# Where the last eight rows of five GpSimd loads go: pairs of rows on chosen DMA engines

## The chip, the cores and the metric

The kernel runs on one core of one Trainium2 chip. The metric is the device time of one execution in microseconds. Three executions of the kernel before took 792.04 to 793.46 us, with a median of 792.78 us.

## The reference, cut to what matters

```python
batch, seq, heads, dim = 16, 512, 16, 64          # q, k: float32 [16, 512, 16, 64]
q1, q2 = q[..., :32], q[..., 32:]                 # cos, sin: [512, 32], over all batches and heads
q_rot = np.concatenate([q1 * cos - q2 * sin, q1 * sin + q2 * cos], axis=-1)
...                                               # k_rot the same way
scores = np.einsum('bshd,bthd->bsht', q_rot, k_rot)   # float32 [16, 512, 16, 512]
```

Both inputs are rotated by position, and each query is multiplied with all 512 keys of its batch and head. The inputs have 33.6 MB each, the result 268 MB, so most of the traffic is the storing of scores.

## The kernel before, in words

**Tiles and staging.** A batch's 512 positions lie on 128 partitions, four neighbouring positions to a partition (`b (p c) h d`), so one load of q or k for a batch is 128 rows of 16 KB, 2 MB in all. The unit of the main loop is a tile: 128 queries (one c of one batch) against the 512 keys, for 16 heads. There are 64 tiles, i = 0 to 63, and tile i belongs to batch i // 4. The scores of a tile fill one staging tile `st`, 128 rows of 32 KB, and L188 stores it with one 4 MB transfer on SyncE's queue (SP). Three staging tiles exist, so ScalarE can begin tile i only when the store of tile i - 3 has landed. Batch 0 is treated in smaller pieces (`early`, L211), which the change does not touch.

**One tile.** In `for p in range(HP)` the function `scores` (L190) makes two matmuls for two heads (L201) and one ScalarE copy from PSUM into `st` (L208). Between them, written out by hand in the dictionary `tr`, stand the transposes (L170) of what later tiles need: at p = 1 and 3 those of q for tile i + 1, copied out by VectorE, and at p = 5 and 6 those of k for tile i + 4, copied out by ScalarE (L185). VectorE makes the rotation in three operations (L149, L150, L154): for q of tile i + 2 in the course of tile i, and at the end of tile i for k of tile i + 5. As every engine works in program order, q of batch b is first touched by VectorE around tile 4b - 2, and k of batch b at the end of tile 4b - 5; TensorE can't get past p = 5 of tile 4b - 4 without that k.

**Loads.** `load` (L113) is called at the end of tile i: q of batch i // 4 + 2 after a tile with i % 4 = 2, k of batch i // 4 + 3 after one with i % 4 = 3. Two buffers each are there for q and k, so a load waits for the last transposes of the batch two before. Most loads are one transfer on SP's queue behind the stores (L122).

**Five loads go through GpSimd.** `RELIEVED` (L74) names q of batches 6, 11 and 15 and k of batches 7 and 12. They go to `load_around` (L86), whose aim is that DMA engine 4 (`SLOW`) gets nothing of them. A transfer that GpSimd issues is spread from a cursor that runs over the 16 DMA engines. So `move_cursor` (L79) issues a tiny transfer of n rows of 16 bytes into `scratch`, which moves the cursor on by n, and `halves` (L94) then issues 120 rows, eight for each of 15 engines from engine 5 on. It cuts each row into two runs of 8 KB. The other eight rows go, for q, through SP (L111) to engines 0 to 7, and for k through GpSimd, with the cursor at 8, to engines 8 to 15, ahead of the 120 rows. In all GpSimd issues 18 transfers: 11 tiny ones, five of 120 rows and two of eight rows.

**Completions.** The framework gives GpSimd's transfers eight semaphores in turn. The ninth transfer takes the semaphore of the first and waits, on GpSimd, until the first has landed. GpSimd does nothing else in the main part of the kernel.

Of the kernel before, what the change touches and what calls it, by code (L numbers as in the profile page):

```python
# [10 lines left out]
def kernel(  # L11
# [8 lines left out]
    nc = tc.nc  # L20
    fp32 = mybir.dt.float32
# [3 lines left out]
    B, S, H, D = q.shape  # L25
    HD = D // 2
    P = 128
# [5 lines left out]
    const_pool = ctx.enter_context(tc.tile_pool(name="const", bufs=1))  # L33
# [37 lines left out]
    batches = {}  # L71

    RELIEVED = {("q", 6): 0, ("k", 7): 1, ("q", 11): 2, ("k", 12): 3, ("q", 15): 4}  # L74
    SLOW = 4
    scratch = const_pool.tile([P, 96], fp32, name="scratch")
    tiny = [0]

    def move_cursor(n):  # L79

        y = tiny[0]
        tiny[0] += 1
        src = bass.AP(q.tensor, 512 * y, [(512, n), (64, 2), (1, 2)])
        nc.gpsimd.dma_start(scratch[:n, 4 * y : 4 * y + 4].rearrange("p (a b) -> p a b", a=2), src)

    def load_around(which, b, t):  # L86

        n, E, F = 120, C * H * D, C * H * D // 2  # L90
        x = RELIEVED[which, b]
        d = dram[which][b]

        def halves(lo, hi):  # L94
            src = bass.AP(d.tensor, d.offset + lo * E + F, [(E, hi - lo), (-F, 2), (1, F)])
            v = t[lo:hi].rearrange("p c e -> p (c e)")
            dst = bass.AP(v.tensor, v.offset + F, [v.ap[0], (-F, 2), (1, F)])
            nc.gpsimd.dma_start(dst, src)  # L98

        if x == 0:  # L100
            nc.gpsimd.inc_swdge_sem([], [], mode="reset_dge_cursor")
        else:

            move_cursor(16 - SLOW)
        if x % 2:
            move_cursor(8)
            halves(n, P)
        move_cursor(SLOW + 1)
        halves(0, n)
        if not x % 2:  # L110
            nc.sync.dma_start(t[n:].rearrange("p c (h d) -> p c h d", h=H), d[n:])  # L111

    def load(which, b):  # L113

        if b >= B:
            return
        t = in_pool.tile([P, C, H * D], fp32, tag=which + "_in", name=which + "_sb")
        batches[which, b] = t
        if (which, b) in RELIEVED:
            load_around(which, b, t)  # L120
        else:
            nc.sync.dma_start(t.rearrange("p c (h d) -> p c h d", h=H), dram[which][b])  # L122
# [100 lines left out]
    with tc.manual_schedule():  # L223
# [15 lines left out]
        for i in range(C):  # L239
# [7 lines left out]
            for p in range(HP):  # L247
# [7 lines left out]
                if p in (2, 6):  # L255
                    m = len(dve) - (4 if p == 2 else 2) - (2 if i == C - 1 else 0)
# [64 lines left out]
```

## Time and profile before

| | |
|---|---|
| median of three executions | 792.78 us |
| the profiled execution | 792.13 us |
| its span, first to last instruction | 790.4 us |
| DMA traffic | 336.18 MB, mean 425 GB/s |
| DMA queue 1 (SP), share of 16 engines | 96.4%, 325.46 MB |
| DMA queue 0 (GpSimd), share of 16 engines | 3.1%, 10.10 MB |
| TensorE busy / ScalarE / VectorE / GpSimd | 684.4 / 562.0 / 544.7 / 11.9 us |
| one 4 MB store, issue to landing, median | 24.7 us |
| one 2 MB load of k on SP, issue to landing, median | 28.3 us |
| 120 rows of q / of k on GpSimd, issue to landing, median | 27.8 / 43.3 us |

The span and the busy times come from one profiled execution, which itself took 792.13 us; 1.7 us of that lie outside the span. "Issue to landing" is the time from the start of the issuing instruction until the last of 16 completion marks, and so includes the wait behind transfers that were issued earlier. Times in the traces are counted from the span's start.

### The profile page before, as it was taken

Reading aid. Unit: us, or ns where it says so; the run is one execution under the profiler, and the core shown is the slowest. Engines: PE = TensorE matmul, PEld = TensorE weight load, DVE = VectorE, ACT = ScalarE, POOL = GpSimd, SP = SyncE. Lnnn points to the kernel's source line nnn. Section 1 sums busy time; section 2 is a strip of 40 time slices with the busy share of each in tenths; the row PEclk is TensorE's granted clock in tenths of the full one; section 3 lists DMA queues with packets and bytes.
Section 4 is the critical chain, followed back from the end, with each engine's and each line's share of the span. In section 5 each row is a group of like instructions: output and inputs, shape, how many; then the busy total and the mean of one; then the engine's idle time right before and its main releaser. Section 6 shows DMA issues by size and latency. Waiting matters only on the chain.

```text
span 790.4 us, 7750 instructions
## 1 busy us (share of the span) xinstructions
PE 684.4 (87%) x3072; PEld 296.4 (38%) x3072; DVE 544.7 (69%) x516; ACT 562.0 (71%) x647; POOL 11.9 (2%) x24
## 2 busy tenths in 40 slices
PE   4989998988988889798996989889899798799960
PEld 2444443433433334343342433334334343344420
DVE  6999988666766678576785767667678487587400
ACT  3888886865857768486785866777577586588770
POOL 0000000000001000000000001000000000000000
PEclk9999999998999999898998989999899899899995
DMA  9999999999999999999999999999999999999997
GB/s 357 417 425 439 429 430 435 425 435 436 429 429 428 413 432 419 433 423 438 433 427 436 426 432 429 422 432 424 430 432 427 436 429 432 430 432 434 432 429 340
DMA packets 18836, 336.18 MB, mean 425 GB/s; under 512 B 2312, under 2 KB 3592, under 8 KB 4616
## 3 DMA queue, kind: packets, MB, share of 16 engines
q1 hardware_dynamic: 16704, 325.46, 96.4%
q0 software_dynamic: 1808, 10.10, 3.1%
q8 instruction: 24, 0.39, 0.2%
q10 hardware_dynamic: 288, 0.13, 0.1%
q14 instruction: 12, 0.10, 0.0%
HBM read 67.24 MB, written 268.44 MB: 425 GB/s over the span
## 4 chain that ended last, share of the span: by engine, by line
DMA 49%; PE 40%; ACT 5%; DVE 3%; issue 1%; ACTq 0%; SPq 0%; DVEq 0%
DMA out_dram<-st 46%; PE ps L201 30%; PE bank L170 10%; ACT st L208 5%; DMA q_sb<-in_q_dram 2%; DVE part L149 1%; DMA early<-in_k_dram 1%; DVE q_sb L150 0%; DVE k_sb L154 0%; DVE k_sb L150 0%; DVE q_sb L154 0%; DVE early L150 0%; DVE kT_t L185 0%; ACTq L316 0%; DVE early L154 0%
## 5 line engine op out<-in xcount | busy, mean ns | idle before, releaser
L208 ACT COPY st<-ps 128x1024 f32<-128x1024 f32 x512 | 495.7, 1020 | 192.6 <-DMA out_dram<-st 109.8
L201 PE MATMUL ps<-kT_t,qT_t 64*128 64x512 f32 x2048 | 544.0, 649 | 67.0 <-ACT st L208 67.0
L201 PEld LDWEIGHTS ps<-kT_t,qT_t 64*128 64x128 f32 x2048 | 183.6, 196 | 256.2 <-issue 133.3
L185 DVE COPY qT_t<-bank 128x512 f32<-128x512 f32 x118 | 81.6, 691 | 193.9 <-PE bank L170 193.9
L170 PEld LDWEIGHTS bank<-ident,q_sb 128*128 128x128 f32 x480 | 54.2, 149 | 99.0 <-issue 96.4
L170 PEld LDWEIGHTS bank<-ident,k_sb 128*128 128x128 f32 x480 | 50.3, 140 | 96.4 <-DVE k_sb L150 39.5
L170 PE MATMUL bank<-ident,q_sb 128*128 128x128 f32 x480 | 85.1, 304 | 0.9 <-PE ps L201 0.9
L170 PE MATMUL bank<-ident,k_sb 128*128 128x128 f32 x480 | 78.5, 286 | 1.6 <-DVE qT_t L185 1.2
L185 ACT COPY kT_t<-bank 128x512 f32<-128x512 f32 x122 | 72.4, 598 | 6.4 <-PE bank L170 6.4
L154 DVE TENSOR_TENSOR k_sb<-k_sb,part 128x1024 f32<-128x1024 f32 x60 | 73.5, 1225 | 2.1
L150 DVE TENSOR_TENSOR q_sb<-q_sb,cos_t 128x1024 f32<-128x1024 f32 x60 | 73.5, 1225 | 2.1
L150 DVE TENSOR_TENSOR k_sb<-k_sb,cos_t 128x1024 f32<-128x1024 f32 x60 | 73.5, 1225 | 2.0
L149 DVE TENSOR_TENSOR part<-q_sb,ss_t 128x1024 f32<-128x1024 f32 x60 | 73.5, 1225 | 2.0
L149 DVE TENSOR_TENSOR part<-k_sb,ss_t 128x1024 f32<-128x1024 f32 x60 | 73.0, 1216 | 0.9 <-DMA k_sb<-in_k_dram 0.7
L154 DVE TENSOR_TENSOR q_sb<-q_sb,part 128x1024 f32<-128x1024 f32 x60 | 72.9, 1216 | 0.0
L170 PE MATMUL bank<-ident,early 128*128 128x128 f32 x64 | 10.5, 315 | 12.4 <-DVE early L154 10.5
L170 PEld LDWEIGHTS bank<-ident,early 128*128 128x128 f32 x64 | 8.3, 161 | 17.4 <-issue 13.4
L149 DVE TENSOR_TENSOR part<-early,ss_t 128x1024 f32<-128x1024 f32 x8 | 9.8, 1222 | 5.8 <-DMA early<-in_k_dram 5.7
L98 POOL DMA_DIRECT2D q_sb<-in_q_dram x3 | 2.3, 752 | 620.2 <-PE bank L170 446.2
L154 DVE TENSOR_TENSOR early<-early,part 128x512 f32<-128x512 f32 x16 | 10.3, 687 | 0.2
L150 DVE TENSOR_TENSOR early<-early,cos_t 128x1024 f32<-128x1024 f32 x8 | 9.8, 1225 | 0.3
L185 ACT COPY qT_t<-bank 128x512 f32<-128x512 f32 x10 | 5.7, 629 | 3.2 <-PE bank L170 3.2
(12 smaller groups left out, 15.9 us busy)
## 6 DMA issues: line engine op xcount, KB each, us to landing
out_dram<-st SPq DMA_DIRECT2D x60, 4096.0 KB, 24.7
k_sb<-in_k_dram SPq DMA_DIRECT2D x13, 2048.0 KB, 28.3
q_sb<-in_q_dram SPq DMA_DIRECT2D x12, 2048.0 KB, 26.5
out_dram<-st SPq DMA_DIRECT2D x16, 1024.0 KB, 13.8
q_sb<-in_q_dram POOLq DMA_DIRECT2D x3, 1920.0 KB, 27.8
k_sb<-in_k_dram POOLq DMA_DIRECT2D x2, 1920.0 KB, 43.3
early<-in_k_dram SPq DMA_DIRECT2D x1, 1536.0 KB
early<-in_q_dram SPq DMA_DIRECT2D x1, 1536.0 KB
```

Source lines behind the costliest of these rows:

```text
L98: nc.gpsimd.dma_start(dst, src)
L149: nc.vector.tensor_tensor(pv, xs, ss, op=mult)
L150: nc.vector.tensor_tensor(xc, xc, cs, op=mult)
L154: nc.vector.tensor_tensor(y, y, z, op=add)
L170: nc.tensor.transpose(bank[:, x, :], src, ident)
L185: copy(out=dst, in_=src)
L201: nc.tensor.matmul(out=po, lhsT=lhs[64 * r : 64 * r + 64, :], rhs=rh, start=True, stop=True)
L208: nc.scalar.copy(out=so, in_=si)
```

## The change

The eight rows leave SP and the fixed groups of engines. Each load now issues its 120 rows first, from engine 5 on, and then four transfers of two rows, each to two neighbouring engines; the table gives the first engine of each pair. A transfer starting at 7 goes to engines 7 and 8, one at 15 to 15 and 0, one at 2 to 2 and 3, one at 9 to 9 and 10. Before each of them stands the tiny transfer that moves the cursor there (two tiny ones, of nine and eight rows, where it has to move by one; none where it stands right). GpSimd now issues 53 transfers: 28 tiny ones, five of 120 rows and 20 of two rows. `scratch` becomes wider for the greater number of tiny transfers.

```diff
-    RELIEVED = {("q", 6): 0, ("k", 7): 1, ("q", 11): 2, ("k", 12): 3, ("q", 15): 4}
-    SLOW = 4
-    scratch = const_pool.tile([P, 96], fp32, name="scratch")
+    RELIEVED = {
+        ("q", 6): (7, 15, 7, 15),
+        ("k", 7): (7, 9, 15, 2),
+        ("q", 11): (7, 15, 2, 7),
+        ("k", 12): (7, 9, 15, 2),
+        ("q", 15): (7, 15, 7, 15),
+    }
+    SLOW, NE = 4, 16
+    scratch = const_pool.tile([P, 224], fp32, name="scratch")
     tiny = [0]
+    cursor = []
...
         n, E, F = 120, C * H * D, C * H * D // 2
-        x = RELIEVED[which, b]
         d = dram[which][b]

-        def halves(lo, hi):
+        def rows(lo, hi, engine):
+            d_n = (engine - cursor[0]) % NE
+            for m in (9, 8) if d_n == 1 else (d_n,) if d_n else ():
+                move_cursor(m)
             src = bass.AP(d.tensor, d.offset + lo * E + F, [(E, hi - lo), (-F, 2), (1, F)])
             v = t[lo:hi].rearrange("p c e -> p (c e)")
             dst = bass.AP(v.tensor, v.offset + F, [v.ap[0], (-F, 2), (1, F)])
             nc.gpsimd.dma_start(dst, src)
-
-        if x == 0:
+            cursor[0] = (engine + min(hi - lo, NE - 1)) % NE
+
+        if not cursor:
             nc.gpsimd.inc_swdge_sem([], [], mode="reset_dge_cursor")
-        else:
-
-            move_cursor(16 - SLOW)
-        if x % 2:
-            move_cursor(8)
-            halves(n, P)
-        move_cursor(SLOW + 1)
-        halves(0, n)
-        if not x % 2:
-            nc.sync.dma_start(t[n:].rearrange("p c (h d) -> p c h d", h=H), d[n:])
+            cursor.append(0)
+        rows(0, n, SLOW + 1)
+        for x, engine in enumerate(RELIEVED[which, b]):
+            rows(n + 2 * x, n + 2 * x + 2, engine)
```

## The prediction, made before the changed kernel was run

> **What bounds the kernel now.** I read the page's slices first, then its chain, the waits, and the timelines of GpSimd and VectorE.
>
> ```profile
> DMA  9999999999999999999999999999999999999997
> GB/s 357 417 425 439 429 430 435 425 435 436 429 429 428 413 432 419 433 423 438 433 427 436 426 432 429 422 432 424 430 432 427 436 429 432 430 432 434 432 429 340
> ...
> DMA 49%; PE 40%; ACT 5%; DVE 3%; issue 1%; ACTq 0%; SPq 0%; DVEq 0%
> ```
>
> The 16 DMA engines are busy from the first slice to the last, at a flat rate: the kernel ends when the slowest engine has moved its bytes. The chain's 40% PE does not contradict this; it passes through matmuls that themselves waited for staging tiles, as the waits show:
>
> ```profile
> POOL q_sb L98 <- PE bank L170: 446.2, 2, 224.0
> ...
> ACT st L208 <- DMA out_dram<-st: 109.8, 42, 5.7
> ...
> DVE part L149 <- DMA k_sb<-in_k_dram: 0.7, 1, 0.7
> ```
>
> ScalarE waits 109.8 us for stores; loads make VectorE wait 0.7 us. So compute runs ahead, by the stores in flight: one lands 24.7 us after issue and moves in 9.7 (8 packets of 1.21 per engine), so about 2.5 are queued. When are the relieved loads issued and used? GpSimd, then VectorE:
>
> ```profile
> 226.37 0.75 POOL L98 DMA_DIRECT2D q_sb<-in_q_dram  x1 [223.98 <-PE bank L170]
> 227.12 1.13 POOL L84 DMA_DIRECT2D scratch<-in_q_dram  x2
> 246.84 0.57 POOL L98 DMA_DIRECT2D k_sb<-in_k_dram  x1 [18.59 <-PE bank L170]
> 247.41 0.57 POOL L84 DMA_DIRECT2D scratch<-in_q_dram  x1
> 247.97 0.76 POOL L98 DMA_DIRECT2D k_sb<-in_k_dram  x1
> ```
> ```profile
> 290.31 1.23 DVE L149 TENSOR_TENSOR part<-k_sb,ss_t 128x1024 f32<-128x1024 f32 x1
> ```
> ```profile
> 535.23 1.23 DVE L149 TENSOR_TENSOR part<-k_sb,ss_t 128x1024 f32<-128x1024 f32 x1 [0.72 <-DMA k_sb<-in_k_dram]
> ```
>
> By the trace's completion marks the 120 rows of k7 landed at 290.19, those of k12 at 535.11: VectorE takes both within 0.12 us. **The relieved k loads have no slack.** The q loads have some: q6 landed at 255.2 and is first used at 268.35.
>
> **What the skill says.** "DMA: Bandwidth & Descriptors", section "Queues, rings and completion order": an engine alternates between the queues that have work, packet by packet. The packet records agree: beside a 32 KB store packet of 1.213 us, an 8 KB packet of queue 0 (0.309) comes every 1.52 us, and even a tiny one every 1.22. Same page, "Why a DMA increments its semaphore by 16 and not by 1": GpSimd's transfers post a completion on all 16 engines whatever their shape, and a small one uses consecutive engines from a cursor. Queue 0 has 400 packets of 4 bytes, 16 for each of 18 transfers and 112 that fill engines without data in the large ones; so every small transfer costs every engine turns. "Latency and other measured facts" calls engines 7 and 15 usually slower; the change puts most rows there. The records carry no engine number, so this trace can't confirm it.
>
> **The price of a small transfer.** Landings before (last mark): q6's 120 rows 255.24, the tiny ones of 12 and 8 rows 257.66 and 259.63, k7's eight rows 263.51, a tiny one 265.93, k7's 120 rows 290.19. The ring serves strictly in order: 2.3 us for a tiny one, 3.9 with data, 24.3 for 120 rows. Two-row pieces do not occur before. Bounds: the tiny one's 2.3 and the eight-row piece's 3.9 (also two 8 KB packets per engine used); I take 3.9.
>
> **The change, part by part.**
>
> *Removed from SP:* three eight-row issues (about 1 us each). SP idles 659.7 us at L188 for ScalarE: 0. *GpSimd's issue time:* 35 more transfers at 0.57 are 20 us on an idle engine: 0 by itself.
>
> *Tiny packets:* 17 more tiny transfers with 2 packets and 18 more data pieces with up to 3, at some 10 ns each, are 0.9 us per engine at most, on the bound.
>
> *Rows moved.* A row is 0.62 us. Before, engines 0 to 7 got 3 of the 40 rows and 8 to 15 got 2. After: 7 and 8 get 8; 15 and 0 get 7; 2 and 3 get 3; 9 and 10 get 2; the rest none. So 8 carries +3.7 us, 7 and 15 +3.1, 0 +2.5; 1, 4, 5, 6 carry -1.9, 11 to 14 -1.2. Sorting the packet records into 16 chains (each packet starts 3 or 4 ns before its forerunner ends), five end between 784.95 and 785.68, eleven between 788.07 and 790.37, on average 787.97. Perfect evening is worth 2.4 us; if the last engine is 2, 3, 9 or 10, nothing.
>
> *Order and waits.* The changed program's order on GpSimd names the wait of each transfer. q6: 120 rows, tiny, pair, tiny, pair, tiny, pair, tiny, then the last pair, which takes the semaphore of the 120 rows: **it is not issued before they land, and GpSimd, in order, holds k7 behind it.** k7's 120 rows then wait for q6's first pair, and its own last pair for its own 120 rows; likewise q11, k12 and q15. Working it out from the landings above:
>
> - q6: 120 rows 255.2; four tiny and three pairs, 9.2 + 11.7 = 20.9, give 276.1; last pair 280.0, against first use at 268.35. VectorE stops 12 us in tile 22, and behind it the copies of q of tile 23, so TensorE stops at p = 5. Then products 2.5, a copy 0.7 and some 4 to the store: 287 instead of 282.0. Store 21 lands at 296.25, so the engines have work: 0 (5 us if that cover were gone).
> - k7: 120 rows released at 261.4 (q6's first pair) and not at 248; in the ring behind everything to 280.0 and a tiny one, 282.3; +24.3 is 306.6; four tiny and three pairs 327.5; last pair 331.4. While the SP loads of q7 and k8 pass (16 KB packets of 0.61), turns are shorter: 4.8 us for q7's eight packets, about half of that for k8's. I take **324**, instead of 290.2.
> - What is late next: k's rotation 3.7, then tile 24 from p = 5 to its store, about 5: store 24 at 333, not 306.44, its first packet 2 later. SP's queue then holds nothing beyond k8's load, whose 16 marks fall between 322.0 and 325.9: dry from 324 to 335, 11 us. If k7 lands at 318, 5; at 326, when the empty SP queue stops holding the ring up, 13. I take 9.5.
> - q11: two more tiny ones stand ahead of its 120 rows, 499.9 + 4.6 = 504.5; five tiny and four pairs give 531.6 (first use 514.2): store 42 near 539, covered by store 41. k12: 533.9 + 24.3 + 24.8 = 583 without short turns, as late against 535.2 as k7 or more: another 9.5.
> - q15: 698.9 + 24.8 = 723.7, used at 709.8: store 58 near 731, when store 57 lands (731.3): 0 to 3, I take 1.
>
> A dry spell is lost for good: every tile needs 10.0 us of compute against 12.1 of DMA with loads, 9.7 without, so engines can't make it up. It also puts the 16 engines in step again, so I take the rows' evening (-2.4 to +1.5) and the tiny packets (+0.9) together at 0.
>
> Sum: 792.13 + 9.5 + 9.5 + 1 = 812.1 us against the profiled execution, which is 0.65 below the median; I forecast **812**.
>
> **Rivals.**
>
> *Not slower: the late pieces stay under the queue's cover.* k7 can land up to 313 (324 less 2, 5 and 3.7) and nothing runs dry. With pairs at 2.3 us, k7 would end at 275.9 + 24.3 + 18.4 = 318.6, less the short turns 7.2: 311. Then only evening and tiny packets count: 792.1 - 2.4 + 0.9 = 790.6, or up to 793 if the last engine isn't relieved. For it: the chain ends so uneven, and 2.5 stores are queued. Against it: the eight-row piece took 3.9, and k's slack is nil. 12%.
>
> *Slower still:* each dry spell 13, and q6 or q15 uncovered too (5 and 3): 792 + 34 = 826. Against it: stores 21 and 57 were in flight. 10%.
>
> *The rows don't go where the table says* (the pairs on other engines): evening fails, the waits stay; the same 812.
>
> **How the numbers follow.** Forecast (803 to 820) 73%, covered 12%, slower still 10%, one spell only (794 to 803) 5%. 0.2%, 1.6 us, is about what a measurement of this kernel can tell from no change: faster 0.07 (the covered case with evening), same 0.05, slower 0.88. Range 795 to 822.
>
> **What would show it.** Right: DMA slices below 9 near 325 to 335 and again some 250 us later; VectorE's L149 on k_sb waiting tens of us; GpSimd's pairs waiting for DMA; the last pair of k7 landing near 324; stores 24 and 44 some 25 us late. Wrong: DMA at 9 throughout and k7 landed by 313; or the loss found as longer packets.

## The result, and the profile after

The changed kernel takes 822.58 us (median of 6 runs, 821.33 to 823.79) against 792.64 for the kernel before in the same session: a ratio of 1.0375, with a 95% interval of 1.0358 to 1.0391. It is slower, as forecast, but by 30 us and not by 20: 10.6 us above the forecast of 812, and 0.6 beyond the range's end. The profiled execution took 821.37 us with a span of 819.6, 29.2 more than before. One run further below, 818.36 us of the kernel with the pairs first, counts as slow and is left out of that kernel's median and ratio.

The page's slices and its chain, in the changed kernel (a slice is 20.5 us here):

```profile
DMA  9999999999999998699999999999499999999998
GB/s 353 420 425 439 431 428 435 431 435 427 435 423 433 423 379 352 283 409 412 432 422 441 421 430 429 428 407 410 204 434 383 432 425 439 414 433 431 431 427 365
...
DMA 50%; PE 30%; DVE 9%; issue 4%; ACT 3%; POOL 1%; ACTq 0%; DVEq 0%; POOLq 0%
```

The row of nines has two holes, at 320 to 340 and at 580 to 600 us. They are what the prediction called dry spells. The GB/s row shows more than the digits do: 379 stands *ahead* of the first hole, in a slice whose digit is 9, so the engines count as busy there and move less. The chain now passes through VectorE (9%), and 4% of it is "issue", time for which the profile shows no wait.

The waits of VectorE, in us: total, how often, longest. Before, its waits for k loads were 0.7 us.

```profile
DVE part L153 <- DMA scratch<-in_q_dram: 37.9, 2, 27.6
DVE part L153 <- DMA k_sb<-in_k_dram: 28.0, 1, 28.0
DVE part L153 <- DMA q_sb<-in_q_dram: 20.0, 2, 10.6
```

Two waits of about 28 us are those for k7 and k12, three of about 10 those for q6, q11 and q15. One k wait and one q wait are put down to `scratch`: a tiny transfer next to the last pair ended about when it did, and the wait goes to what came last by the profile. The timelines of VectorE and of SP in the changed kernel, then of SP in the kernel before (start, duration, what it waited for):

```profile
279.49 1.23 DVE L153 TENSOR_TENSOR part<-q_sb,ss_t 128x1024 f32<-128x1024 f32 x1 [10.58 <-DMA q_sb<-in_q_dram]
...
321.08 1.23 DVE L153 TENSOR_TENSOR part<-k_sb,ss_t 128x1024 f32<-128x1024 f32 x1 [27.59 <-DMA scratch<-in_q_dram]
```
```profile
260.81 28.56 SPq L192 DMA_DIRECT2D out_dram<-st  x3
289.47 1.42 SPq L126 DMA_DIRECT2D q_sb<-in_q_dram  x1
299.05 0.33 SPq L192 DMA_DIRECT2D out_dram<-st  x1
299.48 1.09 SPq L126 DMA_DIRECT2D k_sb<-in_k_dram  x1
333.95 10.35 SPq L192 DMA_DIRECT2D out_dram<-st  x2
```
```profile
296.42 0.33 SPq L188 DMA_DIRECT2D out_dram<-st  x1
296.86 1.07 SPq L122 DMA_DIRECT2D k_sb<-in_k_dram  x1
306.44 27.01 SPq L188 DMA_DIRECT2D out_dram<-st  x3
```

k7 is used at 321.08, 30.8 us later than before. After k8's load, issued at 299.48, SP issues nothing until 333.95, when store 24 comes (before: 306.44). That load, the last thing in its queue, lands between 323.96 and 325.75.

Where do 29.2 us lie? I added up all packet records and divided by 16. Per engine, time without a packet grew from 2.1 us to 22.6, **20.5 us of dry time**; time with a packet grew from 788.3 to 797.0, **8.7 us of longer or additional packets**, though the bytes are the same. The windows view shows both kinds (columns: window, length, busy of each engine with instruction counts, PEclk, DMA share, GB/s; a packet counts where it starts, so a share can pass 1); first the changed kernel, then the kernel before:

```profile
290.00:292.00 2.00, 2.00 (x11) 0.70 (x9) 2.00 (x3) 1.48 (x2) 0.00 (x0) 1.00 1.02 287
292.00:294.00 2.00, 2.00 (x12) 1.11 (x12) 0.90 (x2) 1.42 (x3) 0.00 (x0) 1.00 1.05 254
...
320.00:340.00 20.00, 12.00 (x52) 5.45 (x52) 18.47 (x18) 8.07 (x10) 0.00 (x0) 0.72 0.52 222
```
```profile
290.00:292.00 2.00, 2.00 (x9) 0.53 (x5) 1.91 (x3) 0.77 (x1) 0.00 (x0) 0.82 0.95 410
292.00:294.00 2.00, 2.00 (x13) 1.07 (x12) 1.97 (x2) 1.91 (x4) 0.00 (x0) 1.00 1.03 442
```

At 290 to 294 the DMA share is full in both kernels, yet only 254 to 287 GB/s pass, against 410 to 442. At 320 to 340 half of the engines' time is empty. Of the 8.7 us, by packet size and place: 2.3 between 280 and 300 and 1.4 between 540 and 560 (k's 8 KB rows, and some stores beside them); 2.1 between 360 and 380 and 1.9 between 620 and 640 (a store and a load some 30 us after each dry spell); 1.1 in tiny and other small packets.

### The profile page after: what moved, and what is told of

Same layout as the page of the kernel before. It is cut to its first block, busy times and chain, and to the rows that moved or that the text cites. A ratio compares the mean times of both kernels' runs of the same rounds, so it can differ in the third digit from the quotient of the medians.

```text
span 819.6 us, 7794 instructions
## 1 busy us (share of the span) xinstructions
PE 677.6 (83%) x3072; PEld 295.9 (36%) x3072; DVE 543.4 (66%) x516; ACT 561.1 (68%) x647; POOL 31.9 (4%) x59
## 4 chain that ended last, share of the span: by engine, by line
DMA 50%; PE 30%; DVE 9%; issue 4%; ACT 3%; POOL 1%; ACTq 0%; DVEq 0%; POOLq 0%
PE ps L205 23%; DMA out_dram<-st 22%; DMA k_sb<-in_k_dram 15%; DMA q_sb<-in_q_dram 7%; PE bank L174 7%; DMA scratch<-in_q_dram 6%; DVE part L153 3%; ACT st L212 3%; DVE early L154 1%; DVE k_sb L158 1%; DVE k_sb L154 1%; DVE early L158 1%; DVE q_sb L154 1%; POOL q_sb L107 1%; DMA sin_t<-in_sin_dram 0%
## 5 line engine op out<-in xcount | busy, mean ns | idle before, releaser
L205 PE MATMUL ps<-kT_t,qT_t 64*128 64x512 f32 x2048 | 534.8, 641 | 42.4 <-ACT st L212 42.1
L205 PEld LDWEIGHTS ps<-kT_t,qT_t 64*128 64x128 f32 x2048 | 181.7, 193 | 223.7 <-issue 140.6
L174 PE MATMUL bank<-ident,k_sb 128*128 128x128 f32 x480 | 82.0, 295 | 65.3 <-DVE qT_t L189 65.3
L174 PEld LDWEIGHTS bank<-ident,k_sb 128*128 128x128 f32 x480 | 52.4, 145 | 161.5 <-DVE qT_t L189 71.1
L107 POOL DMA_DIRECT2D q_sb<-in_q_dram x15 | 9.0, 602 | 580.4 <-PE bank L174 353.9
L92 POOL DMA_DIRECT2D scratch<-in_q_dram x28 | 16.2, 578 | 50.9 <-DMA q_sb<-in_q_dram 37.7
L158 DVE TENSOR_TENSOR early<-early,part 128x512 f32<-128x512 f32 x16 | 10.3, 687 | 0.2
```

The source lines that it names most:

```text
L158: nc.vector.tensor_tensor(y, y, z, op=add)
L174: nc.tensor.transpose(bank[:, x, :], src, ident)
L205: nc.tensor.matmul(out=po, lhsT=lhs[64 * r : 64 * r + 64, :], rhs=rh, start=True, stop=True)
```

## The experiments

The prediction's theory, **R**: GpSimd's ring (its packets waiting at the DMA engines) is served in order, one packet to a turn beside the stores; the small transfers make q6 and then k7 late; when k is later than the queue's cover (the stores and loads still in flight), SP's queue runs dry. Its rivals: **P**, the placement on engines 7, 8, 15 and 0 costs by itself; **W**, the semaphore wait of the last pair is what makes it late, not the ring's sum. Later a question was added: what makes packets longer (8.7 us).

### Small transfers without any row moved

Two kernels: the kernel before, with rows where they were, and 14 or 6 tiny transfers without use behind the 120 rows of q6 and q11.

```diff
+    EXTRA = 14
...
         halves(0, n)
+        if which == "q" and b < 15:
+            for _ in range(EXTRA):
+                move_cursor(8)
```

> The kernel before with its rows where they were; behind the 120 rows of q6 and of q11 stand 14 more tiny cursor transfers of eight rows, which carry no data of the computation. Theory R (GpSimd's ring serves its transfers one after the other, 2.3 us for a tiny one, and k lands behind all of them): k7 lands near 290.2 + 14 x 2.3 = 322, less some 5 where SP loads shorten the turns, so 317 to 320; the DMA engines run dry for 4 to 10 us at k7 and again at k12, 800 to 815 us in all. If the longer packets seen in the changed kernel follow from a dry spell, the load after each spell shows them here too, about 2 us each. Rival P (the loss comes from where the rows go, engines 7, 8, 15 and 0): 792 to 794, as no row moves.

> The same with 6 tiny transfers instead of 14. Theory R: k7 lands near 290.2 + 14 = 304, which is later than before but earlier than 313, where the stores in flight stop covering it: no dry spell, 791.5 to 794 us. A loss in proportion to the transfers (a cost of the tiny packets themselves) would give 6/14 of what 14 cost, 796 to 802. Rival P: 792 to 794.

Measured: with 14, 824.04 us (ratio 1.0387, 1.0372 to 1.0403); with 6, 796.46 (1.0039, 1.0025 to 1.0054). With 14, k7 landed at 322.65 and VectorE used it as late as in the changed kernel:

```profile
322.77 1.23 DVE L153 TENSOR_TENSOR part<-k_sb,ss_t 128x1024 f32<-128x1024 f32 x1 [35.39 <-DMA k_sb<-in_k_dram]
```

With 6 it landed at 305.15, VectorE waited 14.0 and 17.0 us for the k loads, and still no dry spell followed (3.1 us without a packet in the whole run). Both times lie above what R had put down (800 to 815 and 791.5 to 794). The 796.46 lies at the edge of the range for a loss in proportion to the transfers, 796 to 802; but 6/14 of the 30.4 us that 14 really cost would be 13, and 2.8 were lost. They are longer packets too (3.3 us in the profiled execution). With 14, the whole loss comes without a single row on another engine: P is not needed for it, and small transfers in k's way are enough. With 14, the dry time is 16 us, and 15.7 us are longer packets; I had not expected those. Between 300 and 311 q7's load on SP and k7's rows ran at once there, with hardly a store beside: 16 KB packets took about 1000 ns instead of 611, 8 KB packets 410 to 530 instead of 309.

### Each half of the change alone

In one kernel q has pairs and k stays as before; in the other k has pairs and q stays. The table of engines, left out here, has 0 or 8 for a load that stays.

```diff
...
+        if RELIEVED[which, b] == 8:
+            rows(n, P, 8)
         rows(0, n, SLOW + 1)
+        if RELIEVED[which, b] == 0:
+            nc.sync.dma_start(t[n:].rearrange("p c (h d) -> p c h d", h=H), d[n:])
+        elif RELIEVED[which, b] != 8:
+            for x, engine in enumerate(RELIEVED[which, b]):
+                rows(n + 2 * x, n + 2 * x + 2, engine)
```

> q6, q11 and q15 send their last eight rows in pairs as in the changed kernel; k7 and k12 send theirs as before, in one transfer to engines 8 to 15 ahead of the 120 rows. Theory R: k7 lands near 279.4 + 2.3 + 3.9 + 2.3 + 24.3 = 312, less 5 for short turns: 307 to 310, under 313, so no dry spell: 790 to 794 us. Rival P: engines 7, 8, 15 and 0 get 5 to 8 of the rows, nearly what they get in the changed kernel: 806 or more. A loss in proportion to the number of small transfers would also give about 806.

> k7 and k12 send their last eight rows in pairs as in the changed kernel; q6, q11 and q15 send theirs through SP as before. Theory R: q6 lands as before near 255, k7's 120 rows near 282 and its last pair near 303 to 307, under 313: no dry spell, 790 to 794 us, though neither half of the change alone is free of late landings. Rival P and a loss in proportion to the number of small transfers: half of the change's loss, about 806.

Measured: pairs for q, 797.41 us (1.0047, 1.0032 to 1.0062); pairs for k, 794.43 (1.0016, 1.0007 to 1.0024). k7 landed at 309.21 and 304.89. Neither has a dry spell (2.1 and 3.3 us without a packet). R had put both at 790 to 794, so the first is 3.4 us too slow and the second 0.4; P and a loss in proportion, at about 806, are far off. Together the halves lose 0.6%, the whole change 3.75%: it is the *sum* of both delays that passes a limit. In the kernel with pairs for q the lost time is in longer packets again: 6.1 us in its profiled execution, 4.9 of them in 8 KB packets, at 475 to 590 ns on average between 288 and 296.

### The placement alone, and a smaller dose

The first kernel gives pairs to q15 only, where no relieved k follows. The second sends one pair to 7 and 8 and one to 15 and 0 for each q, the other four rows through SP, and leaves k as before. Its edit, without the table:

```diff
...
+        if which == "k":
+            rows(n, P, 8)
         rows(0, n, SLOW + 1)
+        if which == "q":
+            nc.sync.dma_start(t[n + 4:].rearrange("p c (h d) -> p c h d", h=H), d[n + 4:])
```

> Only q15 sends its last eight rows in pairs, to engines 7, 8, 15 and 0; the other four loads send theirs as before. No k load stands behind it, so theory R has no dry spell. It measures the evening alone, with the engines' lead kept to the end: engines 1 to 6 get one row less, 7, 8, 15 and 0 one or two more; 0 to 1 us less than before if the last engine is one of 1 to 6, otherwise the same: 791.5 to 794. Rival P (rows on 7, 8, 15 and 0 slow these engines): 8 of 40 rows, 6 us slower, 798 or more.

> For q6, q11 and q15 one pair of rows to engines 7 and 8 and one to 15 and 0 through GpSimd, after the 120 rows, and the other four rows through SP; k7 and k12 as in the kernel before (their eight rows ahead). Worked out from the ring's order and prices: q6 complete at 267.6, just within its use at 268.35; k7 near 300 instead of 290, late by 10 against a limit of 20 or so: no dry spell. If that holds, 791 to 795, with at most 1 us gained by the evening. If the placement itself costs, or small transfers cost even where nothing is late, above 797.

Measured: 793.38 us for the first (1.0003, 0.9995 to 1.0011), 793.26 for the second (1.0000, 0.9992 to 1.0008). In the second, q6's last row landed at 267.37 and VectorE did not wait for it; k7 landed at 298.29 with a wait of 11.4 us, and nothing ran dry. So rows on the engines that the table calls 7, 8, 15 and 0 cost nothing that can be measured, at 8 and at 12 rows of the 30 that the changed kernel puts there. P had put even 8 rows at 6 us, and the two halves together move all the rows for 0.6%: P falls. Which engine a row really went to, no record tells. The rows bring nothing either. The last 30 us of the first kernel have 2.84 us without a packet instead of 3.65, so its chains end 0.8 us more evenly, but q15's pairs are late too and leave 1.9 us dry at 720 to 740.

### The pairs ahead of the 120 rows

The changed kernel with the order turned round. No pair then has to wait for the 120 rows of its own load.

```diff
-        rows(0, n, SLOW + 1)
         for x, engine in enumerate(RELIEVED[which, b]):
             rows(n + 2 * x, n + 2 * x + 2, engine)
+        rows(0, n, SLOW + 1)
```

> The changed kernel with each load's four pairs ahead of its 120 rows and not behind them. The last pair no longer takes the semaphore of the 120 rows, so no pair waits for them; the ring carries the same transfers. Theory R: the sum of the ring is the same, k7 lands last with its 120 rows, near 325: 820 to 828 us. Rival W: the waits of 23 to 25 us on GpSimd are gone, so the loss goes to half or less, under 808.

Measured: 804.89 us, widely spread (802.86, 804.89 and 812.87; 1.0174, 1.0126 to 1.0223). By the number W is right (under 808), and R's 820 to 828 misses. But the long wait did not go, as was expected; it moved. k7's last pair now takes the semaphore of q6's 120 rows, and k7's 120 rows stand behind it:

```profile
280.77 0.56 POOL L107 DMA_DIRECT2D k_sb<-in_k_dram  x1 [24.59 <-DMA q_sb<-in_q_dram]
...
289.26 0.76 POOL L107 DMA_DIRECT2D k_sb<-in_k_dram  x1 [3.08 <-DMA k_sb<-in_k_dram]
```

Here the waits do bind for some 2 us: when k7's 120 rows are issued at 289.26, SP's queue is empty too, and the DMA share at 288 to 290 is 0.29. Until about 296 the ring then had hardly a turn to share with stores, about half of the 120 rows moved by then, and k7 landed at 313.21 and not near 325, with no dry spell behind it. This execution, the fastest, lost 3.5 us without a packet, at 280 to 300 and at 540 to 560, and 7.3 us in longer packets. So the run does not decide between R and W for k7. For q6, none of whose transfers waits for its 120 rows any more, it does: q6 was used at 280.56, no earlier than in the changed kernel (279.49). For the changed kernel itself GpSimd's timeline decides:

```profile
257.72 0.56 POOL L107 DMA_DIRECT2D q_sb<-in_q_dram  x1 [24.95 <-DMA q_sb<-in_q_dram]
...
263.57 0.77 POOL L107 DMA_DIRECT2D k_sb<-in_k_dram  x1 [3.48 <-PE ps L205]
```

The last pair of q6 is issued at 257.72 after 24.95 us of waiting, as foretold; but the ring works on the earlier small transfers until 276.85, so it would not have been served sooner. It is the same for k7: its last pair is issued at 305.90, and the transfers ahead of it in the ring land until 319.17. The wait is there and isn't what binds.

### A late k without any GpSimd traffic added

Loads exactly as before; VectorE makes products without use ahead of the first product for k7 and k12 (25 or 10 of them), or for q6 and q11 (10).

```diff
+    STALL = {28: 25, 48: 25}
...
         def products():
+            for _ in range(STALL.get(n, 0) if which == "k" else 0):
+                nc.vector.tensor_tensor(pv, ss, ss, op=mult)
             nc.vector.tensor_tensor(pv, xs, ss, op=mult)
```

> The kernel before with all its loads as they are; VectorE makes 25 products of 1.23 us more (values that the next product overwrites, so work without use) ahead of the first product for k7 and for k12. These then begin about 31 us later, at 321 and 566, as late as in the changed kernel (321.1), with no added GpSimd traffic. If a late k alone makes the loss, SP's queue must run dry for about 10 us twice: 793 + 20 = 813. If the longer packets of the store and the load after a dry spell belong to the dry spell itself (all engines set in step), 2 us more for each: 817. If they belong to GpSimd's traffic, 813. If the loss of the changed kernel has another cause than the lateness of k, less than 803. The longer 8 KB packets of 280 to 300 must be absent in any case, so 822 is not reached.

> As the kernel with 25 added products, but with 10: the first product for k7 and k12 begins 12.3 us late, near 302.6 and 547.5, and the store behind it about as much, near 318. By the prediction's limit (313 for k7) the queue still holds work: no dry spell, so neither dry time nor the longer packets behind it, and 793 to 795. If any lateness of k costs its own length, about 817; if the cover is smaller than the limit says, 796 to 805.

> The kernel before with all its loads as they are, and 10 products more (12.3 us) ahead of the first product for q6 and q11, which then begin near 280, as late as in the changed kernel (279.5). The prediction put this lateness at 0 because store 21 covers it. With the loads as before, store 21 lands at 292 to 296 and the late store 22 comes near 288: covered, 793 to 794. If q's lateness by itself empties SP's queue, 2 to 5 us each time: 797 to 803.

Measured: k late with 25 products 824.46 us (1.0389, 1.0369 to 1.0408); with 10, 793.33 (0.9999, 0.9991 to 1.0008); q late with 10, 795.04 (1.0021, 1.0011 to 1.0031). VectorE and the slices of the kernel with 25, then the slices of the kernel with 10 for k:

```profile
DMA  9999999999999996699999999999399999999998
...
290.10 31.44 DVE L151 TENSOR_TENSOR part<-ss_t 128x1024 f32<-128x1024 f32 x25
321.57 1.22 DVE L152 TENSOR_TENSOR part<-k_sb,ss_t 128x1024 f32<-128x1024 f32 x1
```
```profile
DMA  9999999999999999999999999999999999999997
...
292.56 12.55 DVE L151 TENSOR_TENSOR part<-ss_t 128x1024 f32<-128x1024 f32 x10
305.15 1.22 DVE L152 TENSOR_TENSOR part<-k_sb,ss_t 128x1024 f32<-128x1024 f32 x1
```

A k7 that is used at 305.15, with k12 as late, costs nothing; one that is used at 321.57, again with k12, costs 31 us for the two: the cover is real, and the lateness of k is by itself enough for the loss. That the total comes so near the changed kernel's 30 us is chance, as its parts differ: here 28 us are dry and not 20, and my two expectations (813 and 817) missed by that. Its stores and loads share no turns with late small transfers, so the engines finish k8's load earlier (marks 320.6 to 325.8 against 323.96 to 325.75), and store 24 is issued 1.8 us later, at 335.75. The longer packets after a dry spell are there as well, with nothing added to the ring: 1.9 us at 360 to 380 and 2.0 at 620 to 640 (after: 2.1 and 1.9). So they don't need late GpSimd traffic. Nor do they need a dry spell: the kernel with pairs for q has 1.4 us of them at 340 to 360. For q, used at 280.99 as in the changed kernel, store 22 was issued at 291.40 and store 21's marks fell between 291.92 and 296.78: no gap in the queue and no slow rows at 288 to 294. The 1.6 us that this kernel loses (793 to 794 were expected) stay unexplained, as its profiled execution, 793.48 us, was its fastest.

### What makes k's rows slow when they run by themselves

At 290 to 294 of the changed kernel almost only GpSimd's rows run (the last packets of store 21 end at 293.26), at 475 to 620 ns for 8 KB on average. Is it the cut into 8 KB, GpSimd's queue, or neither? Two kernels load k1 and q1 at the start, before any store, in 8 KB runs, on SP's queue or on GpSimd's. A third is the kernel with pairs for q, with the 120 rows of k7 and k12 in whole rows of 16 KB (these rows are spread otherwise than before). The edit of the second:

```diff
+        elif b == 1:
+            E, F, d = C * H * D, C * H * D // 2, dram[which][b]
+            v = t.rearrange("p c e -> p (c e)")
+            src = bass.AP(d.tensor, d.offset + F, [(E, P), (-F, 2), (1, F)])
+            dst = bass.AP(v.tensor, v.offset + F, [v.ap[0], (-F, 2), (1, F)])
+            nc.gpsimd.dma_start(dst, src)
```

> The kernel before, with the loads of k and q of batch 1, at the start, where no stores run yet, in two runs of 8 KB per row, second half first, on SP's queue. If the packet form makes an 8 KB packet long where no stores lie between (627 ns at most in the kernel with pairs for q, 309 beside stores), its 8 KB packets take 450 to 630 ns here, and the start a few us more; if that belongs to GpSimd's queue, they take about 309. The time as a whole: 792 to 797.

> The same two loads in the same 8 KB runs, issued by GpSimd at the start. If the form or GpSimd's queue makes the packets long without stores between, 450 to 630 ns; if neither does, about 309. Together with the same rows on SP's queue this tells form from queue. They may also run beside the loads of SP's queue for batch 0, where two loads at once would lengthen both. The time as a whole: 792 to 798.

> As the kernel with pairs for q alone, but k7's and k12's 120 rows in one packet of 16 KB per row. There SP's queue holds no store from 288 to 294 and the rows of k7 run by themselves, in 8 KB packets of 475 to 627 ns instead of 309. If the cut into 8 KB makes them long, the 16 KB packets take 611 here; if GpSimd's rows by themselves are slow whatever their form, 1000 to 1250. The time, with the rows of k spread otherwise, is not what this run is for: 795 to 812.

Measured, one execution each: 793.08, 801.41 and 804.23 us. At the start the 8 KB packets took 309 ns on SP's queue and 309 to 328 on GpSimd's (6 to 14 us: 408 to 433 GB/s), though GpSimd's rows had the engines almost to themselves. (801.41 missed its range because batch 0's loads then come behind those rows, and the engines stand idle for 5.6 us at 20 to 40.) In the third kernel the 16 KB packets took 1009 ns on average at 290 to 292 and 1184 at 292 to 294 instead of 611:

```profile
290.00:292.00 2.00, 2.00 (x12) 1.11 (x12) 1.79 (x3) 1.48 (x3) 0.00 (x0) 1.00 1.03 287
292.00:294.00 2.00, 2.00 (x12) 0.91 (x10) 1.28 (x2) 1.76 (x2) 0.00 (x0) 1.00 0.97 229
```

That is the same rate as with 8 KB packets. So the cut is not the reason, and GpSimd's queue by itself isn't either. Nor is running without stores: in the changed kernel k8's load on SP's queue has the engines to itself at 321 to 323, in the middle, and its 16 KB packets take 616 ns. What makes GpSimd's rows slow at 290 to 294 is not settled by these runs.

### Whole rows in every GpSimd transfer

Fewer packets might shorten the ring's work: beside a store packet of 1.21 us a turn would take some 1.8 us with a 16 KB packet (an estimate, 1.21 and 0.61) and takes 1.5 with an 8 KB one. Both kernels were tried with 16 KB runs:

```diff
-            src = bass.AP(d.tensor, d.offset + lo * E + F, [(E, hi - lo), (-F, 2), (1, F)])
+            src = bass.AP(d.tensor, d.offset + lo * E, [(E, hi - lo), (1, E)])
             v = t[lo:hi].rearrange("p c e -> p (c e)")
-            dst = bass.AP(v.tensor, v.offset + F, [v.ap[0], (-F, 2), (1, F)])
+            dst = bass.AP(v.tensor, v.offset, [v.ap[0], (1, E)])
```

> The changed kernel with every row of its GpSimd transfers as one run of 16 KB, where it is two of 8 KB. Same transfers, same engines, same order and waits. Theory R (the ring takes one packet per turn, and between two of them stands a 1.21 us store packet): 120 rows take 8 turns of 1.82 us, 14.6 us and not 24.3, and a pair 3.0 and not 3.9. q6 is complete near 270, k7 at 272 + 14.6 + 21.2 = 308 less short turns, 303 to 306, under 313: no dry spell, and no GpSimd load running without stores beside it, so no longer packets: 789 to 793 us. Rival W (the wait of the last pair for its own 120 rows, and GpSimd's order behind it, are what costs): the waits are the same 13 to 14 of them, so most of the loss stays, 810 to 820. Rival P (the placement): 820.

> The kernel before with every row of its GpSimd transfers as one run of 16 KB. Theory R: k7 and k12 land 10 us earlier than before, which nobody waits for; 791 to 794, no difference. It serves to tell the evening of the rows from the form of the packets: what the changed kernel with whole rows gains beyond this one is the placement's.

Measured: the changed kernel 807.66 us (1.0178, 1.0164 to 1.0191), the kernel before 809.98 (1.0214, 1.0200 to 1.0228). Both expectations missed. k7 did come earlier, at 304.73 in the changed kernel, and there was no dry spell behind it. But 10.3 and 11.0 us are without a packet in the last 30 us (before: 3.65); the rest of either loss, 5.8 and 5.5 us, is longer packets. In the kernel before with whole rows 15 of the last store's 16 marks fall between 796.35 and 797.32, and one at 806.00: a single engine ends almost a whole store behind the others. So it would look if the relief of one engine, at which the kernel before aims, were lost. The Trainium skill has a possible reason in "DMA: Bandwidth & Descriptors", "Why a DMA increments its semaphore by 16 and not by 1": GpSimd spreads some direct copies over 16 engines with a share of rows rounded up for each, whatever the cursor says. 120 rows would then lie on engines 0 to 14, and engine 4 would get its eight. The one late engine fits that; the records carry no engine number, so no run here shows which it is, nor how the rows were spread.

## Why the prediction was right in kind and too small

**q6 late: right in size, in part by luck.** Last pair predicted at 280.0, landed at 279.41; VectorE stopped for 10.6 us (12 predicted). The 120 rows landed 2.2 us later than was taken (257.43), and the eight small transfers behind them took 22.0 us and not 24.8.

**k7 late: right.** Its 120 rows were predicted at 306.6 and landed at 305.61; the last pair at 324, landed at 320.90. k12's wait is as long (28.0), as said.

**The two dry spells: right.** Store 24 was predicted at 333 and issued at 333.95, where two errors cancel: k7 came 3.1 us earlier than the 324, and from its landing to the store it took 13.1 us and not 8.7. Of 9.5 us predicted for each, 10.7 per engine are empty between 320 and 360, and again 10.7 between 580 and 620. q15 was to cost 1 and shows no dry spell: store 58 was issued at 756.71, before store 57 had landed at 760.02. With a more even end (2.63 us without a packet in the last window instead of 3.65) and the start, empty time grew by 20.5 us; predicted were 20.

**The limit of about 313: not contradicted.** k7 at 309.21 (pairs for q), a k used at 305.15 (10 products) and even k7 at 313.21 (pairs first) stayed without a dry spell behind them; 320.90 was over. But with the measured 13.1 us in place of 8.7 the same sum gives some 309, and in the kernel with the pairs first the cover itself came later: k8's load landed until 330.32. A single limit, taken from one schedule, is too simple.

**The bold sentence on the last pair's wait: right in fact, wrong in weight.** The wait of 24.95 us is there, but the ring's sum sets the time; q6 is as late with the wait gone.

**The ends of the 16 chains** lie at 783.6 to 789.0 us on the trace's clock, 1.4 us earlier than the prediction gives them. It used only their differences, and these are right.

**Where it failed: the term that I took at 0.** The prediction said that engines fall in step and "so I take the rows' evening (-2.4 to +1.5) and the tiny packets (+0.9) together at 0", and it had no term for packets that get longer; these stood only in its last line, as what would make it wrong. Measured, that term is +8.7 us; the 1 us of evening is counted within the 20.5. The 8.7 are of three kinds:

- 4.0 us behind the two dry spells. The kernel with 25 products shows as much without added traffic. The six dry spells of three traces (the changed kernel, 25 products, 14 tiny transfers) each cost their length and 1.8 to 2.1 us more.
- 3.7 us where k's rows run by themselves at 280 to 300 and at 540 to 560. This is a second failing step, the one on q6: "Store 21 lands at 296.25, so the engines have work: 0 (5 us if that cover were gone)." I took store 21's landing from the trace of before. In the changed kernel k7's rows, which had shared its turns, come later, so store 21's marks fall at 288.96 to 293.26, while store 22 is issued only at 289.03. The cover moved with the change. The gap did not show as dry, because k7's rows filled it, at about two thirds of the rate. In the kernel with q late and loads as before, store 21's last mark fell at 296.78 and the cover held.
- 1.1 us in tiny and small packets (0.9 predicted at most).

With 8.7 in place of 0, and 20.5 in place of 20, the prediction's sum is 792.1 + 29.2 = 821.3, the profiled execution's 821.37. It closes because both parts are counted in that very trace; it tells where the time lies, not why packets are longer. The rival "slower still" gave 826 by another way, longer dry spells, and that isn't what happened.

**What stays open.** Why a store and a load some 30 us behind a dry spell take 2 us more, and why GpSimd's rows run at half to two thirds of the rate by themselves in the middle of the kernel and at full rate at its start. The Trainium skill reports in "DMA: Bandwidth & Descriptors", "Latency and other measured facts", that copies whose rows lie a large power of two apart lose bandwidth, and gives channel aliasing of streams in lockstep as an inference. The engines are in step after a dry spell: in the kernel with 25 products the marks of the store issued at 345.89 lie within 0.8 us of each other, those of stores in the kernel before some 4 us apart. But the page's clear losses begin at 2 MiB between rows (at 512 KiB it has 207 GB/s of 214), and here rows lie 128 KB apart in a store and 16 KB in a load. So it is a weak candidate for the first question. No run here changed a pitch.

No version that was tried beats the kernel before: the best are level with it.

## What to carry to other kernels

Price a small transfer on GpSimd's queue by what it puts ahead of the next large one: here 1.8 to 4.3 us of ring time each behind q6's rows, paid by k7, a load to which they don't belong. In this kernel a late load cost 0 to 3.7 us as long as stores in flight covered it, and 30 us once two k loads came later than that, so two nearly harmless halves can make a harmful whole; work out the cover, and take the landings that form it from the *changed* schedule, not from the trace of before. And when the time of a dry spell is estimated, add the rate at which the queue runs around it: busy engines can be slow ones, and GB/s shows what the DMA share hides.

## What the hardware showed unexpectedly

- Packets get longer around changes of traffic: 8 KB from 309 to between 475 and 620 ns on average when GpSimd's rows run almost without stores in the middle of the kernel; 16 KB from 611 to about 1000 ns when two loads run at once with few stores. Beside stores, in turns, they kept 309 and 611.
- Whether a GpSimd row is one packet of 16 KB or two of 8 KB changes how evenly the engines end, and costs the kernel before 17 us with the same bytes: one of 16 engines then ends 8.7 us behind the other 15.
- Rows on the engines that the table calls 7, 8, 15 and 0 cost nothing that can be measured, 8 or 12 of them (1.0003 and 1.0000).
